# A two-block transformer kernel: two gate units move later in the mixture of experts, and the second attention mixer gets a written order with keys on partitions

## The chip, the core and the metric

The kernel runs on one core of one Trainium2 chip, in one launch. The metric is the device time of that launch in microseconds (us). A core has five engines that run side by side: TensorE (PE, matmuls and transposes; its weight loads are counted apart as PEld), VectorE (DVE), ScalarE (ACT), GpSimd (POOL) and SyncE (SP). SP issues nearly all the DMAs here, in the order of its own queue. Each engine takes its instructions in order; between engines they wait for semaphores.

## The reference, cut to what matters

The sequence has 512 tokens of 1024 features. Two blocks follow each other; the change is in the second, whose two layers are:

```python
for i in range(2):
    mix = even_mixer(x, ...) if i == 0 else odd_mixer(x, ...)
    x   = layer_norm(ALPHA * x + mix @ w_o[i], ln1_g[i], ln1_b[i])
    ffn = expert_choice_moe(x, router_w[i], w1[i], w3[i], w2[i])
    ple = sigmoid(x @ ple_gate_w[i] + ple_gate_b[i]) * (p[i] @ ple_w[i])
    x   = layer_norm(ALPHA * x + ffn + ple, ln2_g[i], ln2_b[i])

def odd_mixer(x):                     # 16 query heads, 4 key/value heads of 64
    q, k, v = split(x @ w_in)         # 1024, 256, 256 columns
    q, k = rope(rms_norm(q)), rope(rms_norm(k))       # per head
    return softmax(q @ k.T / 8) @ v                   # no mask, 512 x 512 scores per head

def expert_choice_moe(x):             # 16 experts, 64 tokens each
    gates, idx = top_k(softmax(x @ router_w).T, 64)
    y = (silu(x[idx] @ w1) * (x[idx] @ w3)) @ w2 * gates   # 1024 x 1024 weights
    return scatter_add(y, idx)
```

## The kernel before, in words

Precision: a float32 matrix is split into a high part (float32r, `whi`) and the rest (`wlo`); a product is then three fast matmuls (`mm3`, L227 to L229: high by high, low by high, high by low). `split` (L218, L221) casts on ACT and subtracts on DVE, or on POOL where `pool` is set or `self.every` divides the count. Matmuls on plain float32 operands (the `ss`, `rt`, `o` products, the expert products) are issued as two passes each, and a float32 operand that is only 64 columns wide lets two heads or two experts sit side by side in the array.

Nothing outside the experts has an order written out by hand. A scheduler with a timeline model orders each engine's instructions by their dependencies and their place in the code; only inside `experts` does `keep_order` chain the PE instructions in the order of the code.

**Experts (`experts`).** Per layer 8 pairs `pi` of experts run one after the other. Each pair is two halves of hidden columns (`half` 0 and 1), each with products `a1`, `a3` (L1647, tile `a`), then transposes `ht`, then two products `y`. The weights come in chunks of 1 MB (`chunk`, L1639), 24 per pair, into 8 rotating slots; a chunk's DMA can be issued when the slot's earlier chunk has been used. `gather` (L1664, tile `ga`) fetches the tokens of four experts, every second pair, by matmuls with one-hot matrices: 16 matmuls for two feature tiles `kk` that share one PSUM tile, with DVE (L1670) taking out `kk = 0` and ACT (L1668) `kk = 1`. `scatter` (L1685, L1686) adds the pair's output to the tokens. Six of the eight `ple` gate units (`unit`, 30 fast matmuls each, tiles `pg`, `pv`, with 0.5 MB of weights of their own) are set between the halves by two tables: `units_a` after half 0, `units_b` after half 1. `ef.close()` at the last pair gives back the memory of the units, and in layer 1 the last norm's gain and bias (`lng`, `lnb`) are then loaded there.

**Between the layers (`next_features`, L1394 to L1398).** 32 transposes bring the normed tokens to features on partitions; ACT applies gain and bias (`xf`), DVE casts to the high part (`h`) and subtracts (`l`), eight tiles. Each key or query projection (tile `qk`) needs all eight.

**Odd mixer (`odd_mixer`).** `normed_rope` projects 128 columns (two heads), squares (`sq`), sums by a matmul (`ss`, L1824), takes the root on ACT (`r`), scales (`z`), rotates by a matmul (`rt`, L1830), and adds the two rope terms on DVE and POOL (L1832 to L1834). There are two such for the keys and eight for the query pairs. `full_pair` is the attention of two heads with queries on partitions: scores `s` (two passes, L1002), their maximum on DVE (L1003), the exponential on ACT with the sum accumulated (L1004), the division on DVE (L281), 32 transposes `pt` (L1016), their copies out of PSUM, and the products `o` with the values (L1027). `xtok * G + Bb` (L1879, L1880) rebuilds the residual on POOL, one whole token tile per pair in the code for the first four pairs.

Of the kernel before, what the change touches and what calls it, by code (L numbers as in the profile page):

```python
# [11 lines left out]
F32 = mybir.dt.float32  # L12
# [20 lines left out]
def constants():  # L33
# [55 lines left out]
    c["before"] = before  # L89
    c["slot"] = np.tile(np.arange(64, dtype=f32)[None, :], (128, 1))  # L90
# [55 lines left out]
class K:  # L146
# [5 lines left out]
    def open(self, es):  # L152
# [12 lines left out]
        nc.sync.dma_start(self.norms, self.ins["norms"].rearrange("p (n k) -> p n k", n=5))  # L165
        eps = p.tile([128, 1], F32, name="eps")
# [142 lines left out]
    def program(self):  # L309
        with ExitStack() as es:  # L310
            self.open(es)
            self.wr = es.enter_context(self.pool("wr", 3))
            for l in range(2):
                with ExitStack() as eB, ExitStack() as eA:
# [11 lines left out]
                    else:  # L326
                        with self.pool("nfg", 1, side="right") as gp, self.pool("wh", 2) as self.wh:
                            w = self.ins["w_in_odd_2"][0]
                            self.every = 99
                            k0 = self.split(self.wcols(w, 1024, 128), True)  # L330
                            gain = self.next_features(gp, A)
                            self.odd_mixer(A, B, k0, *gain)
# [696 lines left out]

    def even_mixer(self, A, B):  # L1030
# [351 lines left out]
    def next_features(self, gp, A):  # L1382
# [3 lines left out]
        with self.pool("nf", 2) as p, self.pool("nfp", 3, PSUM) as pp:  # L1386
# [3 lines left out]
            G, Bb = self.ln_load(gp, 0, "ln2")  # L1390
            for k in range(8):
# [3 lines left out]
                f = p.tile([128, T], F32, name="xf")  # L1395
                nc.scalar.activation(f, ps, AF.Identity, scale=g[:, k:k + 1], bias=b[:, k:k + 1])
                nc.vector.tensor_copy(A[0][k], f)
                nc.vector.tensor_sub(A[1][k], f, A[0][k])  # L1398
        return G, Bb
# [175 lines left out]
    def keep_order(self, first):  # L1575

        nc, tc = self.nc, self.tc
        prev = None
        for i in nc.cur_bb.bb.instructions[first:]:
            if i.engine == nc.tensor.engine:  # L1580
                if prev is not None:
                    tc.add_manual_dep(i, prev.name, mybir.DependencyInfo(mybir.DependencyClass.NoSync, mybir.DependencyReason.DATA),
                                      reason="keep_order")
                prev = i

# [34 lines left out]
    def experts(self, l, xhl, aff, slT, slot, g, b, st, ef, r1, early):  # L1620
# [3 lines left out]
        with ExitStack() as es:  # L1624
# [31 lines left out]
            def gather(xg, OH, k2s):  # L1656

                for k2 in k2s:
                    ps = pp.tile([128, 2, 256], F32, name="ga", tag=("t", "y", "sc", "y")[k2])
                    for kk in range(2):  # L1660
# [6 lines left out]
                        if kk:  # L1667
                            nc.scalar.activation(xg[:, k], ps[:, kk], AF.Identity, scale=g[:, k:k + 1], bias=b[:, k:k + 1])  # L1668
                        else:
                            nc.vector.tensor_scalar(xg[:, k], ps[:, kk], g[:, k:k + 1], b[:, k:k + 1],  # L1670
                                                    op0=OP.mult, op1=OP.add)
# [121 lines left out]
    def odd_mixer(self, A, B, k0, G, Bb):  # L1793
# [3 lines left out]
        with ExitStack() as es:  # L1797
# [55 lines left out]
            for j in range(8):  # L1853
                if j == 2:
                    self.every = 1
# [46 lines left out]
```

## Time and profile before

| | us |
|---|---|
| median of 3 runs (lowest, highest) | 3506.03 (3505.88, 3511.51) |
| the profiled execution, its own time | 3509.84 |
| its span, first to last instruction | 3508.0 |
| experts of layer 0, from the first gather | 2128 to 2642 |
| between the layers and odd mixer | 2642 to 2885 |
| output product, norm, routing of layer 1 | 2885 to 2971 |
| experts of layer 1, from the first gather | 2971 to 3485 |

The page cuts the span into 40 slices of 88 us. A digit is the busy share in tenths. PE is near 9 almost everywhere, which by itself says little: matmuls overlap, and an engine that waits for data between them still looks busy. The DMA line tells the stages apart: low shares in the first two thirds, 9 in both stages of experts. PEclk is the granted clock of TensorE in tenths of full speed.

### The profile page before, as it was taken

Reading aid. Unit: us, or ns where it says so; the run is one execution under the profiler, and the core shown is the slowest. Engines: PE = TensorE matmul, PEld = TensorE weight load, DVE = VectorE, ACT = ScalarE, POOL = GpSimd, SP = SyncE. Lnnn points to the kernel's source line nnn. Section 1 sums busy time; section 2 is a strip of 40 time slices with the busy share of each in tenths; the row PEclk is TensorE's granted clock in tenths of the full one; section 3 lists DMA queues with packets and bytes.
Section 4 is the critical chain, followed back from the end, with each engine's and each line's share of the span. In section 5 each row is a group of like instructions: output and inputs, shape, how many; then the busy total and the mean of one; then the engine's idle time right before and its main releaser. Section 6 shows DMA issues by size and latency. Waiting matters only on the chain. (4 is left out here: it accounts for less than half of the span.)

```text
span 3508.0 us, 37612 instructions
## 1 busy us (share of the span) xinstructions
PE 3305.6 (94%) x15018; PEld 2155.8 (61%) x15018; DVE 1582.8 (45%) x2527; ACT 1070.3 (31%) x1933; POOL 510.7 (15%) x357
## 2 busy tenths in 40 slices
PE   8999999999999999999989889999997999999996
PEld 6666578888766657888866765344435657444342
DVE  6555463444555546344457753122216775211213
ACT  4333333223333333322355432011013553111011
POOL 2012121001101212100230423000003103100001
PEclk9999999999999999999999989999998998999998
DMA  5101132234210113233220225999992013899997
GB/s 183 48 25 61 37 110 81 96 96 137 75 60 13 61 36 106 77 96 96 90 86 3 72 102 227 407 412 386 417 421 85 28 43 113 366 408 378 421 407 301
DMA packets 223583, 584.85 MB, mean 167 GB/s; under 512 B 17584, under 2 KB 160304, under 8 KB 173232
## 3 DMA queue, kind: packets, MB, share of 16 engines
q1 hardware_dynamic: 222976, 581.66, 43.9%
q8 instruction: 118, 1.93, 0.2%
q10 hardware_dynamic: 432, 0.79, 0.1%
q14 instruction: 57, 0.47, 0.0%
HBM read 580.30 MB, written 2.10 MB: 166 GB/s over the span
## 5 line engine op out<-in xcount | busy, mean ns | idle before, releaser
L218 ACT CAST whi<-w 128x1024 fp32r<-128x1024 f32 (+1 forms) x312 | 311.2, 1003 | 731.7 <-PE mm L228 498.8
L1647 PE MATMUL a<-w,xg 128*64 128x512 f32 x2048 | 481.4, 600 | 42.2 <-DMA w<-in_w_dram 42.2
L227 PE MATMUL mm<-h,whi 128*128 128x512 f32 x1056 | 417.9, 396 | 4.8 <-ACT whi L218 4.1
L229 PE MATMUL mm<-h,wlo 128*128 128x512 f32 x1056 | 415.0, 394 | 0.4 <-POOL wlo L221 0.3
L228 PE MATMUL mm<-l,whi 128*128 128x512 f32 x1056 | 412.0, 390 | 0.0
L221 DVE TENSOR_TENSOR wlo<-w,whi 128x1024 fp32r<-128x1024 f32 (+1 forms) x237 | 306.4, 1297 | 233.8 <-ACT whi L218 232.5
L1647 PEld LDWEIGHTS a<-w,xg 128*64 128x64 f32 x2048 | 158.5, 138 | 348.6 <-issue 252.8
L221 POOL TENSOR_TENSOR wlo<-w,whi 128x1024 fp32r<-128x1024 f32 x75 | 166.2, 2218 | 642.4 <-ACT whi L218 445.0
L1647 PE MATMUL y<-w,hT 128*64 128x512 f32 x1024 | 226.3, 594 | 3.3 <-DMA w<-in_w_dram 3.3
L227 PEld LDWEIGHTS mm<-h,whi 128*128 128x128 f32 x1056 | 199.3, 189 | 48.1 <-ACT whi L218 5.3
L229 PEld LDWEIGHTS mm<-h,wlo 128*128 128x128 f32 x1056 | 199.0, 188 | 47.2 <-DVE wlo L221 1.0
L228 PEld LDWEIGHTS mm<-l,whi 128*128 128x128 f32 x1056 | 199.0, 188 | 44.7 <-issue 0.7
L602 DVE TENSOR_REDUCE mx<-s 128x1 f32<-128x128 f32 x192 | 93.3, 489 | 192.6 <-PE s L601 191.7
L1742 DVE SCALAR_TENSOR_TENSOR th<-th,a 128x512 f32<-128x512 f32 x32 | 22.0, 688 | 317.5 <-ACT th L1741 317.5
L1647 PEld LDWEIGHTS y<-w,hT 128*64 128x64 f32 x1024 | 72.4, 137 | 144.8 <-issue 136.3
L604 ACT ACTIVATE P<-s,mx 128x128 f32<-128x128 f32 x192 | 100.9, 527 | 174.5 <-DVE mx L602 162.3
L948 POOL TENSOR_TENSOR u<-u 128x512 f32<-128x512 f32 x64 | 66.6, 1040 | 521.4 <-ACT E L947 275.5
L1717 POOL TENSOR_TENSOR og<-OH,aff 128x512 f32<-128x512 f32 x16 | 16.8, 1047 | 764.2 <-DVE oT L1760 747.6
L1785 DVE SCALAR_TENSOR_TENSOR yl<-y,gate,yh 128x512 fp32r<-128x512 f32 x32 | 24.0, 751 | 223.3 <-ACT yh L1784 223.3
L959 DVE TENSOR_TENSOR y<-mm,r 128x512 f32<-128x512 f32 x64 | 44.2, 691 | 160.8 <-PE mm L229 160.8
L1741 ACT ACTIVATE th<-a 128x512 f32<-128x512 f32 x32 | 19.1, 597 | 319.8 <-PE a L1647 319.8
L621 PEld LDWEIGHTS pt<-c_ident,P 128*128 128x128 f32 x480 | 54.8, 145 | 73.1 <-issue 63.9
(584 smaller groups left out, 6414.2 us busy)
## 6 DMA issues: line engine op xcount, KB each, us to landing
w<-in_w_dram SPq DMA_DIRECT2D x384, 1024.0 KB, 12.6
w<-in_w_in_dram SPq DMA_DIRECT2D x32, 1024.0 KB, 5.3
w<-in_w_up_dram SPq DMA_DIRECT2D x32, 1024.0 KB, 5.5
w<-in_w_down_dram SPq DMA_DIRECT2D x32, 1024.0 KB, 5.1
w<-in_w_out_dram SPq DMA_DIRECT2D x8, 1024.0 KB, 5.2
w<-in_w_o_dram SPq DMA_DIRECT2D x8, 1024.0 KB, 4.7
w<-in_ple_gate_w_dram SPq DMA_DIRECT2D x16, 512.0 KB, 4.9
w<-in_w_in_even_dram SPq DMA_DIRECT2D x7, 1024.0 KB, 5.4
```

What stands on the lines that cost most here:

```text
L218: nc.scalar.copy(h, view)
L221: e.tensor_sub(l, view, h)
L227: mm(ps, wh, xh, start=first, stop=False)
L228: mm(ps, wh, xl, start=False, stop=False)
L229: mm(ps, wl, xh, start=False, stop=last)
L602: nc.vector.tensor_reduce(mx[:, i:i + 1], s[:, :n], axis=X, op=OP.max, negate=True)
L604: nc.scalar.activation(pv, s[:, :n], AF.Exp, bias=mx[:, i:i + 1], accum_out=sums[:, i:i + 1])
L621: nc.tensor.transpose(ps[:, (i - k) * 128:(i - k + 1) * 128], P[h][0][i][:, k * 128:(k + 1) * 128], C["ident"])
L948: nc.gpsimd.tensor_mul(u, u, u)
L959: nc.vector.tensor_mul(y, ps, r2)
L1647: nc.tensor.matmul(ps[64 * a:64 * a + 64], lhs(a, 4 * kc + k), cw[a][:, k], start=kc == 0 and k == 0, stop=kc == 1 and k == 3)
L1785: nc.vector.scalar_tensor_tensor(yl, y, gate, yh, op0=OP.mult, op1=OP.subtract)
```

## The change

1. **Gather.** DVE and ACT take out both halves of a gather tile after all 32 of its matmuls, not each after its own 16; the two engines change roles by name only.
2. **Gate units.** `units_a` goes from {0: 2, 3: 5} to {3: 4, 7: 7} and `units_b` from {0: 3, 2: 4, 4: 6, 6: 7} to {0: 2, 2: 3, 4: 5, 6: 6}: pair 0 has one unit instead of two, the last pair has one after its first half. The memory is given back after the last pair, and `lng`, `lnb` are loaded then.
3. **Between the layers.** Four PSUM tiles and four `xf` buffers; the casts `h` alternate between ACT and DVE; the residual scaling no longer stands here. The first key weights and the first query weights are both loaded and split ahead of it, on POOL. The two small norm gains are loaded at the program's start.
4. **Odd mixer.** Scores are computed twice: once with queries on partitions from the high parts only, for the maximum (`max_steps`), and once with keys on partitions (`attend_steps`), where the second pass carries the negative maximum in four spare rows. The exponential then gives the transposed weights directly; the sums come from adding the four key tiles (`acc`, two adds of three on POOL) and one matmul with ones; the division is done on the output, with a logarithm and an exponential on ACT. No transposes of the weights are left. `weave` sets the order of the steps from a string, and `keep_order` fixes it on PE.
5. **Residual.** Half a token tile per pair, all eight pairs, on POOL, each behind the output division of its pair.

```diff
@@ open
+        for g, n in zip(self.gqk, ("gqa_q_norm_2", "gqa_k_norm_2")):
+            for b in range(2):
+                nc.sync.dma_start(g[64 * b:64 * b + 64], self.ins[n][0].rearrange("(a b) -> a b", b=1))
@@ max_steps
+        def one(i):
+            s = pp.tile([128, T], F32, name="s", tag="s")
+            nc.tensor.matmul(s, q[:, 128 * i:128 * i + 128], k, start=True, stop=True)
+            nc.vector.tensor_reduce(mt[:, r0 + i:r0 + i + 1], s, axis=X, op=OP.max, negate=True)
+        def spread():
+            ps = pp.tile([128, 128], F32, name="mt", tag="mm")
+            nc.tensor.transpose(ps, mt, C["ident"])
+            rows = slice(r0, r0 + 4)
+            nc.vector.tensor_tensor(dst[rows]..., ps[rows, None, :]..., C["diag4"][rows]..., op=OP.mult)
@@ attend_steps
+        def score(h, k):
+            s = pp.tile([128, T], F32, name="st", tag="t")
+            for n, (kk, qq) in enumerate(passes[h]):
+                nc.tensor.matmul(s, kk[:, 128 * k:128 * k + 128], qq, start=n == 0, stop=n == len(passes[h]) - 1)
+            pt = PT[h, k] = at.tile([128, T], F32, name="PT", bufs=6)
+            nc.scalar.activation(pt, s, AF.Exp)
+            if k == 0:
+                acc[h] = at.tile([128, T], F32, name="acc")
+            else:
+                e = nc.vector if k == 3 else nc.gpsimd
+                e.tensor_add(acc[h], PT[h, 0] if k == 1 else acc[h], pt)
+        def norm():
+            nc.scalar.activation(r, sm, AF.Ln)
+            nc.scalar.activation(r, r, AF.Exp, scale=-1.0)
+            self.done = nc.vector.tensor_mul(r, r, o[0])
+            self.put_split(B, j, r)
@@ next_features
-            G, Bb = self.ln_load(gp, 0, "ln2")
-                nc.vector.tensor_copy(A[0][k], f)
+                (nc.vector.tensor_copy if k % 2 else nc.scalar.copy)(A[0][k], f)
@@ experts
-                        if kk:
-                            nc.scalar.activation(xg[:, k], ps[:, kk], AF.Identity, ...)
-                        else:
-                            nc.vector.tensor_scalar(xg[:, k], ps[:, kk], ...)
+                    k = 2 * k2
+                    nc.vector.tensor_scalar(xg[:, k], ps[:, 0], ...)
+                    nc.scalar.activation(xg[:, k + 1], ps[:, 1], AF.Identity, ...)
-            units_a, units_b = {0: 2, 3: 5}, {0: 3, 2: 4, 4: 6, 6: 7}
+            units_a, units_b = {3: 4, 7: 7}, {0: 2, 2: 3, 4: 5, 6: 6}
@@ odd_mixer
-                o = pp.tile([128, T], F32, name="o", tag="o", bufs=1)
-                self.full_pair(at, pp, o, passes, V)
-                self.put_split(B, j, o)
-                if j < 4:
-                    xt = self.xtok[:, j]
-                    nc.gpsimd.tensor_mul(xt, xt, G)
-                    nc.gpsimd.tensor_add(xt, xt, Bb)
+            self.weave("kkkkkkkk pp k pppppp k vvv p v k v p k v v vv", k=ks, p=p0, v=late)
+            self.weave("pp mp mp m mp mp mpp m m m p m", m=tops, p=steps[:9])
+                self.weave("pp r aa p aa pp mm aa p mm vv m m p aa p m vv mm p s s m kkkkkkkk kkkk", **chains)
+                s = slice(512 * (j % 2), 512 * (j % 2) + 512)
+                xt = self.xtok[:, j // 2, s]
+                m = nc.gpsimd.tensor_mul(xt, xt, G[:, s])
+                self.tc.add_manual_dep(m.ins, self.done.ins.name, ..., reason="residual")
+                nc.gpsimd.tensor_add(xt, xt, Bb[:, s])
```

In the strings p is one step of a query projection (eight triples of matmuls, then `ss`), r the rotation `rt` with the split of the next queries, a a score step, m a maximum step, v the values' product, s the sums and the division, k a step of the keys.

How the program's order moves, at three places. First SP, which issues the DMAs, in the experts of layer 1, last four pairs before and after (w is an expert chunk of 1 MB, `in_ple_gate` a unit's weights). Before:

```order
L1697 DMA w<-in_ple_gate_w_dram 128x1024
L1639 DMA w<-in_w_2_dram 128x2048 x48
L1697 DMA w<-in_ple_gate_w_dram 128x1024
L1639 DMA w<-in_w_2_dram 128x2048 x8
L1378 DMA lng<-in_ln_g_dram 128x1024
L1378 DMA lnb<-in_ln_b_dram 128x1024
L1639 DMA w<-in_w_2_dram 128x2048 x24
```

and in the change:

```order
L1773 DMA w<-in_ple_gate_w_dram 128x1024
L1717 DMA w<-in_w_2_dram 128x2048 x16
L1773 DMA w<-in_ple_gate_w_dram 128x1024
L1717 DMA w<-in_w_2_dram 128x2048 x8
L1469 DMA lng<-in_ln_g_dram 128x1024
L1469 DMA lnb<-in_ln_b_dram 128x1024
L1717 DMA w<-in_w_2_dram 128x2048 x8
```

The last pair's 24 chunks stood behind `lng` and `lnb`; now only its last 8 do, and a unit's weights stand between its first and second half.

Second, POOL from the end of layer 0's experts into the odd mixer (wlo is a split, z the rope term, xtok the residual). Before:

```order
L1717 TENSOR_TENSOR og<-OH,aff 128x512 x6
L221 TENSOR_TENSOR wlo<-w,whi 128x1024 x2
L1879 TENSOR_TENSOR xtok<-xtok,lng 128x1024 x4
L1880 TENSOR_TENSOR xtok<-xtok,lnb 128x1024 x4
L1833 TENSOR_TENSOR z<-z,c_gc 128x512 x2
```

and in the change, one pair of the loop (the third) on POOL:

```order
L228 TENSOR_TENSOR wlo<-w,whi 128x1024
L2022 TENSOR_TENSOR xtok<-xtok,lng 128x512
L1916 TENSOR_TENSOR z<-z,c_gc 128x512
L2025 TENSOR_TENSOR xtok<-xtok,lnb 128x512
L1969 CAST Q_17611<-z 64x512
L1969 CAST Q_17612<-z 64x512
L1097 TENSOR_TENSOR acc<-PT 128x512 x2
L1097 TENSOR_TENSOR acc<-acc,PT 128x512 x2
```

All eight residual instructions stood in one block ahead of the first rope; now two of them, at half the size, stand around each pair's rope term, and the adds of the sums are new behind them.

Third, PE in a pair of the odd mixer. Before, the piece around the fourth pair's sum of squares:

```order
L1016 MATMUL pt<-c_ident,P 128x128 x8
L1002 MATMUL s<-kh_17640,Q_18004 128x512
L1002 MATMUL s<-kl_17641,Q_18004 128x512
L1824 MATMUL ss<-sq,c_ones_17587 128x512
L1002 MATMUL s<-kh_17640,Q_18004 128x512
L1002 MATMUL s<-kl_17641,Q_18004 128x512
L1016 MATMUL pt<-c_ident,P 128x128 x4
L1027 MATMUL o<-PT,vo 64x256 x5
```

and in the change, the end of the second pair:

```order
L1069 MATMUL s<-kh_17772,Q_18088 128x512
L1103 MATMUL o<-PT,vo 64x512 x4
L1069 MATMUL s<-kh_17772,Q_18088 128x512 x2
L1906 MATMUL ss<-sq,c_ones_17596 128x512
L1108 MATMUL sm<-acc,ones 64x512 x2
L1074 MATMUL mt<-c_ident,mt_17601 128x128
```

The sum of squares `ss` is the same in both. The transposes `pt` are gone; the maximum's scores `s`, the sums `sm` and the small transposes `mt` are new, and nothing may pass them.

## Rows read from the trace of the kernel before

**Rows 1.** The page's 40 slices: granted clock and DMA share, in tenths.
```profile
PEclk9999999999999999999999989999998998999998
DMA  5101132234210113233220225999992013899997
```
**Rows 2.** Windows of the stages: busy us of each engine, granted clock, DMA share, GB/s.
```profile
2170.00:2642.00 472.00, 438.83 (x2034) 195.03 (x2030) 95.86 (x151) 52.17 (x88) 11.02 (x8) 1.00 0.99 406
2642.00:2709.00 67.00, 48.93 (x212) 36.19 (x211) 43.02 (x49) 23.76 (x39) 28.29 (x12) 0.77 0.16 50
2709.00:2885.00 176.00, 168.91 (x842) 105.69 (x840) 130.32 (x244) 102.56 (x219) 27.92 (x16) 0.99 0.11 37
```
**Rows 3.** Windows of 10 us in the experts, columns as before.
```profile
2150.00:2160.00 10.00, 10.00 (x48) 4.64 (x47) 1.38 (x2) 1.16 (x2) 3.10 (x3) 1.00 0.57 215
2160.00:2170.00 10.00, 10.00 (x49) 5.73 (x49) 2.67 (x4) 1.78 (x4) 1.05 (x1) 1.00 0.65 263
2250.00:2260.00 10.00, 10.00 (x49) 3.42 (x50) 0.75 (x1) 1.42 (x3) 0.00 (x0) 1.00 0.77 297
2380.00:2390.00 10.00, 9.68 (x50) 4.20 (x52) 0.42 (x2) 1.73 (x3) 0.00 (x0) 1.00 0.34 125
...
3220.00:3230.00 10.00, 8.72 (x55) 5.28 (x55) 1.09 (x2) 1.82 (x4) 0.00 (x0) 1.00 0.34 142
```
**Rows 4.** What PE waited for ahead of its gather matmuls (us, times).
```profile
  DVE xg L1670: 54.8, 64
```
**Rows 5.** PE in the experts of layer 0: start us, us, instruction, idle before.
```profile
2157.48 0.50 PE L227 MATMUL pg<-xfh,whi 128*128 128x512 f32 x1
...
2164.42 0.60 PE L1755 MATMUL ot<-c_ident,og 128*128 128x128 f32 x4
2164.95 13.95 PE L1647 MATMUL a<-w,xg 128*64 128x512 f32 x64
...
2602.51 15.01 PE L1647 MATMUL a<-w,xg 128*64 128x512 f32 x64
...
2623.81 3.65 PE L1647 MATMUL y<-w,hT 128*64 128x512 f32 x16 [0.35 <-DMA w<-in_w_dram]
2628.78 3.65 PE L1647 MATMUL y<-w,hT 128*64 128x512 f32 x14 [1.31 <-DMA w<-in_w_dram]
```
**Rows 6.** DVE between the layers: start us, us, instruction.
```profile
2657.53 0.42 DVE L1397 CAST h<-xf 128x512 fp32r<-128x512 f32 x1
2657.98 0.69 DVE L1398 TENSOR_TENSOR l<-xf,h 128x512 fp32r<-128x512 f32 x1
2658.59 2.58 DVE L1397 CAST h<-xf 128x512 fp32r<-128x512 f32 x1
2661.21 2.75 DVE L1398 TENSOR_TENSOR l<-xf,h 128x512 fp32r<-128x512 f32 x1
```
**Rows 7.** POOL between the layers and at one rope term.
```profile
2658.06 10.64 POOL L1879 TENSOR_TENSOR xtok<-xtok,lng 128x1024 f32<-128x1024 f32 x4 [5.94 <-PE xt L1394]
2668.66 10.35 POOL L1880 TENSOR_TENSOR xtok<-xtok,lnb 128x1024 f32<-128x1024 f32 x4
2685.82 1.29 POOL L1833 TENSOR_TENSOR z<-z,c_gc 128x512 f32<-128x512 f32 x1 [6.81 <-PE rt L1830]
```
**Rows 8.** PE at the first key projection's end, and single costs in the loop.
```profile
2675.13 0.63 PE L229 MATMUL qk<-h,wlo 128*128 128x512 f32 x1
...
2709.11 0.40 PE L1002 MATMUL s<-kl,Q 128*128 128x512 f32 x1
2709.35 0.40 PE L1002 MATMUL s<-kh,Q 128*128 128x512 f32 x1
...
2725.37 1.08 PE L1027 MATMUL o<-PT,vo 128*64 128x256 f32 x8
...
2745.02 1.02 PE L1824 MATMUL ss<-sq,c_ones 128*128 128x512 f32 x2
```
**Rows 9.** SP at the program's start.
```profile
1.66 0.43 SPq L291 DMA_DIRECT2D xT<-in_xT_dram  x1
```

More of the change, by code (lines that the diff above doesn't have):

```diff
@@ L1028, in full_pair, with weave @@
                                          start=k == 0, stop=k == 3)
+    def weave(self, plan, **chains):
+        at = dict.fromkeys(chains, 0)
+        first = len(self.nc.cur_bb.bb.instructions)
+        for c in plan:
+            steps = chains.get(c, [])
+            if c == " " or at.get(c, 0) >= len(steps):
+                continue
+            at[c] += 1
+            steps[at[c] - 1]()
+        assert all(at[c] == len(x) for c, x in chains.items()), (at, {c: len(x) for c, x in chains.items()})
+        self.keep_order(first)
@@ L1385, in next_features @@
         x = self.xtok
[L1386 removed]
+        with self.pool("nf", 2) as p, self.pool("nfp", 4, PSUM) as pp:
             cols = gp.tile([128, 16], F32, name="cols2")
@@ L1852, in odd_mixer @@
-            keys(0)
-            for j in range(8):
-                if j == 2:
-                    self.every = 1
-                if j == 3:
-                    keys(1)
-                if j % 2 == 0:
-                    raw = self.wcols(w, 128 * j)
-                z = normed_rope(raw[:, :, (j % 2) * 128:(j % 2) * 128 + 128], gq)
-                if j == 0:
-                    self.token_major(pp, w[:, 1280:1536], XH, XL, [v[:, t] for t in range(4)], one, "t")
+                z = []
+                steps = normed_rope((lambda: self.wcols(w, 1024 + 128 * j, 128)) if j else (lambda: first[0]), gk, z, "mm" if j else "s")
@@ L1863, in odd_mixer, with weights, project, queries @@
+            raws, zq, passes = {0: qw}, {}, {}
+            def weights(j):
+                if j % 2 == 0 and j:
+                    raws[0] = self.wcols(w, 128 * j)
+                return raws[0][:, :, (j % 2) * 128:(j % 2) * 128 + 128]
+            def project(j):
+                zq[j] = []
+                return normed_rope((lambda: weights(j)) if j else (lambda: first[1]), gq, zq[j], "mm" if j else "s")
+            def queries(j):
+                z = zq.pop(j)[0]
                 kh, kl = KS[j // 2]
-                passes = []
+                passes[j], steps = [], []
@@ L1872, in odd_mixer @@
+            tops = []
+            ks, p0, vs = keys(0), project(0), []
+            late = [lambda: vs.extend(values())] + [lambda t=t: vs[t]() for t in range(8)]
+            self.weave("kkkkkkkk pp k pppppp k vvv p v k v p k v v vv", k=ks, p=p0, v=late)
+            tops = queries(0)
+            steps = project(1)
+            self.weave("pp mp mp m mp mp mpp m m m p m", m=tops, p=steps[:9])
+            G, Bb = self.ln_load(gp, 0, "ln2")
+            for j in range(8):
                 g = j // 2
@@ new lines, in odd_mixer @@
+                if j < 7:
+                    turn, steps = steps[9], project(j + 2) if j < 6 else []
+                    tops = []
+                    chains["r"] = [lambda: (turn(), tops.extend(queries(j + 1)))]
+                    chains["m"] = [lambda i=i: tops[i]() for i in range(10)]
+                    chains["p"] = steps[:9]
+                if j == 1:
+                    chains["k"] = keys(1)
+                self.weave("pp r aa p aa pp mm aa p mm vv m m p aa p m vv mm p s s m kkkkkkkk kkkk", **chains)
```

169 lines of the change are left out of this document (114 added, 55 removed).

## The prediction

> **What bounds the kernel now.** I read the page's 40 slices first, because they tell the stages apart [rows 1]: the DMA share is 9 in two stretches, the experts of layer 0 and of layer 1, and low elsewhere. The windows by stage come next [rows 2]. In the experts the DMA engines are busy 0.99 of the time and move 406 GB/s; PE waits for weights there, and what counts is only when the DMA engines stand idle. In the odd mixer's pair loop (2709 to 2885) the DMA share is 0.11, the clock 0.99 and PE is busy 168.9 of 176.0 us: PE sets the time. Between the two (2642 to 2709) no engine is full, PE has 48.9 of 67.0 us and a granted clock of 0.77, so for nearly half of the stretch matmuls run at 1.2 GHz and not 2.4: a chain of waits sets it. So the change has three stages with three different limits, and I price each by its own.
>
> **Experts.** Windows of 10 us show where the DMA engines were idle in layer 0 [rows 3]: 4.3 and 3.5 us in the first pair (shares 0.57 and 0.65), 2.3 us at 2250, 6.6 us at 2380, together 16.7 us. Slots were full then and PE had not used them. Layer 1 shows the same dips, the deepest again 0.34.
>
> The gather waits are the first thing removed. PE waited 54.8 us for `xg` in 64 waits [rows 4]; a layer has 16 gather tiles, 32 in all, each seen once on PE and once on PEld, so a tile loses about 0.86 us and a gather of four tiles 3.4 us. Both halves now go out after both are filled, and the next tile is another one in PSUM, so this goes. It is worth something only where the DMA engines stood still: the 2.3 us at 2250 vanish, of the 6.6 us at 2380 about 3.2 remain (a unit at pair 2 and one at pair 3 still stand there).
>
> The unit after the first pair's first half is next. It ran from 2157.48 to 2164.42, 6.9 us [rows 5], exactly where the DMA engines had their first idle stretches. Without it and without the gather waits PE is some 11 us earlier there, and of 7.8 us idle I leave 1 us for the four chunks that the second gather delays. The first two gather tiles come before the DMA engines restart at all: 2 x 0.86 = 1.7 us more. Recovered per layer: 6.8 + 2.3 + 3.4 + 1.7 = 14.2 us.
>
> The same 6.9 us come back in the last pair. There the second half's products took 15.01 us against 13.95 us undisturbed, and PE waited 0.35 and 1.31 us in `y` [rows 5]: a slack of 2.7 us, so some 4.2 us of the unit show at the end of each layer. The unit's weights only change place in the DMA queue. In layer 1 `lng` and `lnb`, 1 MB together, no longer stand ahead of the last 24 chunks; two chunks, 2 MB, take 4.97 us there, so this is at most 2.5 us, and as PE sets the last pair then, I count 1 us. Sum for both layers: 2 x (14.2 - 4.2) + 1 = 21 us gained; bounds 6 (if only the first pair's idle time goes) and 30.
>
> **Between the layers.** DVE's cast took 0.42 us and its subtraction 0.69 us until POOL began the residual; from then on each took 2.58 and 2.75 us [rows 6], six of them in a row (three of each), while POOL did eight instructions in 10.64 + 10.35 us [rows 7]. The two engines took turns, one instruction each. The eight tiles cost DVE 5 x (0.42 + 0.69) + 3 x (2.58 + 2.75) = 21.5 us. The first key projection needs all eight tiles and ended at 2675.8 [rows 8]. In the change four casts are ACT's, the residual is gone from here, and DVE has 4 x 0.42 + 8 x 0.69 = 7.2 us in place of these 21.5. That would give 14 us. Two things take some back: POOL has both first splits and 24 memsets here, and ACT has twelve instructions in place of eight. I take 12 us; bounds 5 and 14. The rest up to the pair loop holds the same projections and the values' product, now in a written order; I count it as equal.
>
> The page SBUF — State Buffer of the Trainium skill, section Who interferes with whom, says that a DVE instruction with two SBUF inputs contends with a GpSimd instruction that reads SBUF, but not with one that only writes it. The turns of rows 6 and 7 agree with the first half; the second would let the memsets pass beside the subtractions, which speaks for the upper end, 14 us. The rule also speaks against this change, further on.
>
> **Pair loop.** First PE's own work, by single costs [rows 8]: a fast matmul of 512 columns starts 0.24 us after the one before, `ss` and `rt` take 1.02 us each, eight passes of `o` at 256 columns 1.08 us. A projection is 24 x 0.24 + 2 x 1.02 = 7.8 us. The loop of before held eight attentions, six query projections and one key projection: (176 - 7 x 7.8) / 8 = 15.2 us for an attention. In the change an attention has 16 fast score matmuls and 8 for the maximum (24 x 0.24 = 5.8 us), 16 passes of values at 512 columns (four times eight passes of half the width in pairs, 2 x 2 x 1.08 = 4.3 us), the sums 1.1 us, two small transposes about 0.4 us: 11.6 us. With its projection a pair is 19.4 us.
>
> Then what waits in the fixed order. The maximum's first scores stand about 6.9 us after the sums of the pair before. Ahead of them on POOL is now the residual's multiplication, which waits for the division of that pair (logarithm, exponential, product: about 2.2 us), then takes about 1.3 us, then the rope term 1.29 us [rows 7]; then DVE's add, ACT's cast and DVE's subtraction, some 0.65 us each, with POOL's second residual instruction of 1.3 us in front of DVE's add: 2.2 + 1.3 + 1.3 + 1.3 + 3 x 0.65 + 0.9 for the steps between = 9 us. So about 2 us of waiting per pair. Behind it PE can do nothing else, since its order is fixed. Six full pairs: 6 x (19.4 + 2) = 128.4; the second keys 7.8, and 4 for their `ss` and `rt`, which stand back to back with nothing between; the seventh pair without projection 11.6 + 2; the last 16 x 0.24 + 4.3 + 1.1 = 9.2, and 1.5 for the exponentials. Together 164.5 against 176, a gain of 11.5 us. Without any wait it would be 25.5, with 4 us per pair a loss of 2.5. The wait of 2 us is the nearest to the rows, as each of its links has one. The residual's eight blocks of two on POOL, 16 x 1.3 = 21 us in all, are otherwise hidden under PE.
>
> **Start.** Four small loads stand ahead of the first token tiles on SP, which takes about 0.45 us for each issue [rows 9]: 1.8 us lost, all of it on the path, since the first matmul waits for those tiles.
>
> **Sum.** 21 + 12 + 11.5 - 1.8 = 42.7 us. The profiled execution took 3509.84 us, 3.8 above the median 3506.03; taken from the median this gives 3463 us. The scheduler also moves instructions in the first block, which the change does not touch; I price that at nothing, with 5 us either way in the range.
>
> **Rivals.**
> 1. *The loop hangs on POOL.* POOL has about 13 us of work in a pair of 20, nearly all of it reading SBUF, and DVE's adds and subtractions on two SBUF operands then take turns with it, as in rows 6. If every one of six such DVE instructions waits 0.7 us more, the wait per pair is 6 us in place of 2, and the loop loses 7 x 4 = 28 us: 3491 us. For it: the turns are in the trace. Against it: DVE has 130 of 176 us now [rows 2] and loses the division and the copies. By the rule of the SBUF page named above this is what should come, for `acc` and the residual both read SBUF. Chance 0.2.
> 2. *The experts give back what they gain.* PE lags in the last pair by the whole unit and the first pair's idle time is set by its 8 slots, not by PE: the gain is 3 us per layer, 3478 us. For it: DMA share 0.99 in the stage. Against it: PE did wait for weights in that pair. Chance 0.15.
> 3. *The clock falls in the loop: slower.* Now PE runs at a granted clock of 0.99 there; in the stretch before, with its waits, it had 0.77 [rows 2]. A fixed order turns each late operand into a wait of all of PE. At half clock a pair's 19.4 us become nearly 39; more than two of the eight pairs at half clock eat the 42.7 us, and four give 3463 + 78 = 3541 us. Against it: waits of 1.31 us in `y` left the clock at full speed [rows 2]. Chance 0.07.
> 4. *No waits.* The written order hides the chain: 14 us more in the loop and 2 before it, 3447 us. Chance 0.2.
>
> The forecast itself has 0.38. About 0.2%, 7 us, is what can be told from no change here. Forecast and rivals 1, 2 and 4 are all faster by more than that, but their errors can reach it: faster 0.90, same 0.04, slower 0.06. The range from 3438 to 3494 holds the forecast's own errors (the bounds of each term) and rivals 1, 2 and 4.
>
> **What would show it.** In the experts: no wait for `xg` inside a gather, DMA shares near 1 from the first pair on, a dip left near the fourth pair, and the last pair's PE without waits for weights. Between the layers: casts at 0.4 and subtractions at 0.7 us, the first key projection ended some 12 us sooner after the last norm. In the loop: no `pt`, about 21 to 22 us from one `ss` to the next, one wait per pair, at the maximum's first `s`, put down to DVE's subtraction into `Q`. Wrong would be a loop of over 176 us, a clock under 0.95 in it, or idle DMA engines in the first pair.

## The result, and the profile after

The changed kernel takes 3450.65 us (median of 4 runs, 3446.95 to 3461.07), the kernel before 3505.95 us beside it; the ratio is 0.9845 with a 95% interval of 0.9818 to 0.9871, 55 us less. Measured once more with the last experiments it was 0.9838 (0.9820 to 0.9857). The forecast was 3463 us, so the sum came out 12 us short of the gain, and some of its terms were off by about as much or more, in both directions.

The profiled execution of after has a span of 3445.2 us, 62.8 below the 3508.0 of before. That is 7.5 more than the medians differ by: the one of before was 3.9 us above its median, the one of after 3.7 below. Cut at the same instructions of PE in both timelines (`affT` ends the routing ahead of a layer's experts, `a` is their first product with weights, `sc` the scatter of their output, `wo` the output product behind the mixer; all in us):

| stretch, by PE's instructions | before | after | gained | priced |
|---|---|---|---|---|
| to the first matmul | 9.1 | 12.1 | -3.0 | -1.8 |
| to the last `affT` of layer 0 (not touched by the change) | 2101.6 | 2089.9 | 11.7 | 0, 5 either way |
| to the first `a` of layer 0, and the same in layer 1 | 23.7 + 24.5 | 21.4 + 21.2 | 5.6 | in the next |
| experts to the last `sc`, layer 0 + layer 1 | 508.5 + 512.5 | 495.8 + 494.6 | 30.6 | 21 |
| last `sc` of layer 0 to the first key projection's end | 32.8 | 18.0 | 14.8 | 12 |
| from there to the first `wo` | 209.2 | 207.9 | 1.3 | 11.5 |
| output product and routing of layer 1, final norm | 86.1 | 84.3 | 1.8 | 0 |

First the page's two lines, which answer to [rows 1].

```profile
PEclk9999999999999999999999989999999999999998
DMA  5101132224310111233321115999994113999997
```

Of the clock's four 8s two are gone, those of slice 31 (between the layers) and of slice 34 (layer 1's routing). The DMA line has a 9 in the first slice of layer 1's experts, where it had an 8. Next the windows that answer to [rows 2] (busy us of PE, PEld, DVE, ACT, POOL; clock, DMA share, GB/s): the experts of layer 0, the stretch between, the pairs.

```profile
2149.00:2619.00 470.00, 440.00 (x2058) 197.74 (x2054) 99.09 (x156) 56.12 (x93) 13.30 (x9) 1.00 0.99 409
2619.00:2673.00 54.00, 43.99 (x221) 34.12 (x220) 32.94 (x52) 24.96 (x44) 22.54 (x31) 0.94 0.21 66
2673.00:2845.00 172.00, 150.87 (x563) 82.74 (x564) 109.53 (x146) 80.60 (x135) 99.58 (x75) 0.97 0.12 42
```

The experts move 409 GB/s in place of 406 at the same share of 0.99, since this window, like that of before, leaves the first pair's start out. The stretch between has a clock of 0.94 in place of 0.77. In the pairs PE's busy time fell from 168.9 of 176.0 to 150.9 of 172.0 us: the work fell by 18 us, the time by 4. POOL has 99.6 us there in place of 27.9.

Three windows of 10 us in layer 0's experts: the first pair, where [rows 3] had shares of 0.57 and 0.65, and two places in the fourth pair with a dip left (before, the deeper one was 0.34).

```profile
2143.00:2153.00 10.00, 10.00 (x50) 3.32 (x48) 1.54 (x2) 0.45 (x1) 1.07 (x2) 1.00 1.01 424
2330.00:2340.00 10.00, 10.00 (x49) 3.57 (x49) 1.45 (x3) 1.05 (x3) 1.05 (x1) 1.00 0.88 346
2350.00:2360.00 10.00, 10.00 (x64) 6.02 (x64) 1.63 (x3) 2.18 (x4) 0.00 (x0) 1.00 0.67 267
```

The first pair's share is full there. At the fourth pair's deeper dip 3.3 us are left idle, where 3.2 were foreseen; a dip of 1.2 us is new in the last pair (share 0.88 from 2580 to 2590), where a unit stands now. PE waits for no `xg` inside a gather any more. The last pair's products `y`:

```profile
2598.07 10.52 PE L1725 MATMUL y<-w,hT 128*64 128x512 f32 x48
```

48 products in one piece, without the waits of 0.35 and 1.31 us of [rows 5]: PE is later than the weights there, as foreseen. Between the layers, DVE (start us, us, instruction, idle before), which answers to [rows 6], and POOL beside it, to [rows 7]:

```profile
2627.98 0.43 DVE L1487 CAST h<-xf 128x512 fp32r<-128x512 f32 x1 [2.18 <-ACT xf L1486]
2628.44 0.69 DVE L1488 TENSOR_TENSOR l<-xf,h 128x512 fp32r<-128x512 f32 x1
...
2629.78 1.90 DVE L1488 TENSOR_TENSOR l<-xf,h 128x512 fp32r<-128x512 f32 x3
...
2633.55 0.78 DVE L1487 CAST h<-xf 128x512 fp32r<-128x512 f32 x1
2634.37 1.29 DVE L1488 TENSOR_TENSOR l<-xf,h 128x512 fp32r<-128x512 f32 x2
```

```profile
2633.56 0.92 POOL L1879 MEMSET mt<- 128x128 f32 x4 [12.16 <-issue]
2634.54 2.23 POOL L1925 MEMSET Q<- 64x512 f32 x4
```

Three of DVE's four casts take 0.43 us and the subtractions 0.63 to 0.69. Beside POOL's memsets (2633.56 to 2636.77) the fourth cast takes 0.78 us, and the last two subtractions take no longer than the others. Last, PE in an ordinary pair, and then in the seventh, the first that has no projection of a later pair between its steps:

```profile
2767.33 0.33 PE L1074 MATMUL mt<-c_ident,mt 128*128 128x128 f32 x1
...
2768.43 0.50 PE L234 MATMUL qk<-h,whi 128*128 128x512 f32 x1 [0.77 <-DVE Q L1076]
...
2775.94 0.73 PE L1069 MATMUL s<-kh,Q 128*128 128x512 f32 x2 [1.04 <-DVE Q L1968]
```

```profile
2809.28 0.33 PE L1074 MATMUL mt<-c_ident,mt 128*128 128x128 f32 x1 [0.55 <-ACT r L270]
...
2812.90 2.05 PE L1913 MATMUL rt<-z,c_rot 128*128 128x512 f32 x2 [3.28 <-DVE z L1910]
...
2813.96 1.42 PE L1090 MATMUL st<-Q,kh 128*128 128x512 f32 x1
...
2819.76 0.74 PE L1069 MATMUL s<-kh,Q 128*128 128x512 f32 x2 [1.25 <-DVE Q L1968]
```

An ordinary pair has the one foreseen wait at the maximum's first `s`, ended by DVE's subtraction into `Q`, and a smaller one at the first projection matmul, which wants the PSUM buffer that DVE's spreading of `mt` still reads. The pairs take 20.66, 20.67, 20.66 us from one `sm` to the next. The seventh takes 22.7 us although it has no projection's 24 matmuls and no `ss`, 6.8 us of PE work less. The record of granted clocks has 1.2 GHz from 2811.4 to 2818.3 there. It fell 1.8 us into the wait of 3.28 us: `rt` takes 2.05 in place of 1.02 us and the first `st` 1.42.

### The profile page after: what moved, and what is told of

Read it like the earlier page. It is cut to its first block, busy times and chain, and to the rows that moved or that the text cites. A ratio compares the mean times of both kernels' runs of the same rounds, so it can differ in the third digit from the quotient of the medians.

```text
span 3445.2 us, 37016 instructions
## 1 busy us (share of the span) xinstructions
PE 3255.6 (94%) x14746; PEld 2111.6 (61%) x14746; DVE 1553.8 (45%) x2435; ACT 1051.8 (31%) x1856; POOL 581.3 (17%) x437
## 5 line engine op out<-in xcount | busy, mean ns | idle before, releaser
L1817 ACT ACTIVATE th<-a 128x512 f32<-128x512 f32 x32 | 19.1, 597 | 341.6 <-PE a L1725 341.6
```

## The experiments

Each is read by its ratio to the kernel before, and by the same cuts as in the table above.

**1. The experts alone.** The kernel before, with these three edits.

```diff
-   if kk: nc.scalar.activation(xg[:, k], ps[:, kk], ...)                   # inside the loop over the halves
-   else:  nc.vector.tensor_scalar(xg[:, k], ps[:, kk], ...)
+   nc.vector.tensor_scalar(xg[:, k], ps[:, 0], ...)                        # behind the loop
+   nc.scalar.activation(xg[:, k + 1], ps[:, 1], ...)
-   units_a, units_b = {0: 2, 3: 5}, {0: 3, 2: 4, 4: 6, 6: 7}     # ef.close(), lng/lnb inside the last pair
+   units_a, units_b = {3: 4, 7: 7}, {0: 2, 2: 3, 4: 5, 6: 6}     # both behind the last pair
```

> The kernel before with the three edits in the experts alone (both halves of a gather tile go out after both are filled; the gate units' new pairs; the late closing of the pool with lng/lnb behind it). Theory from the two traces: the stage's gain is DMA idle time won back, nothing is lost in the last pair, and it needs nothing from the mixer: layer 0 from 508.5 to about 496 us, layer 1 from 531.3 to about 513 us, the first gather tiles some 2 us each; about 35 us in all, 3471 us, ratio 0.990. Rival, the sizes of the prediction: 21 us, 3485 us, ratio 0.994, with PE some 4 us late in each last pair. First two blocks: same order as before, so the times there differ from before only as two executions of one order differ.

Measured: 3467.92 us, ratio 0.9888 (0.9872 to 0.9905), 33 to 45 us. Layer 0 takes 495.95 us, layer 1 496.42. The theory's size holds; 21 us lies outside.

**2 and 3. Each half of it alone.** Gather only, then units with the late closing only.

> The kernel before with the gather edit alone (both halves of a tile filled, then both read). Both theories: no wait for xg inside a gather; the DMA dip of 2.3 us at the second gather goes, of the 6.6 us at the fourth pair about 3.2 stay, the first pair keeps most of its dip since its unit still stands there. About 9 us per layer, 18 us in all, 3488 us, ratio 0.995. If gather waits were covered by the weights' transfers: under 4 us in all, ratio above 0.999.

Measured: 3476.48 us, ratio 0.9911 (0.9896 to 0.9926), 26 to 36 us. The 18 us of both theories were too low.

> The kernel before with the new pairs of the gate units and the late closing alone; the gather as before. Theory from the traces: the first pair's unit of 6.9 us goes from a place where the DMA engines stood idle to a last pair where they set the time, so most of 5 us per layer is won and nothing given back: about 12 us, 3494 us, ratio 0.9966. Rival, the prediction's sizes: 5.1 us won and 4.2 us given back at the end of each layer, 1 us for lng/lnb: 3 us, ratio 0.999, with PE working on without a wait for weights in the last pair and the last products ending 4 us after the last chunk's usual time.

Measured: 3494.57 us, ratio 0.9966 (0.9953 to 0.9979), 7 to 16 us. The total is the theory's, but its places are not:

| kernel | layer 0 | its pairs 1 to 7 | its pair 8 | DMA idle before the last expert weight | from that weight to the end | layer 1 |
|---|---|---|---|---|---|---|
| before | 508.5 | 444.1 | 64.4 | 17.7 | 9.7 | 512.5 |
| gather only | 496.1 | 431.6 | 64.5 | 6.1 | 9.8 | 496.6 |
| units only | 508.0 | 440.0 | 68.0 | 14.8 | 10.5 | 505.1 |
| both, kernel before | 495.95 | 426.9 | 69.0 | 4.6 | 10.4 | 496.4 |
| the change | 495.75 | 426.8 | 69.0 | 4.4 | 10.3 | 494.6 |

(The pairs are cut at PE's first `a` of each. The idle time is the time from the first `a` of layer 0 to the last packet of an expert weight, less that of all DMA packets as a share of 16 engines.) The gather edit alone brings both layers to within 0.2 us of both edits together: on top of it the units' move is worth nothing in these cuts. PE reaches the last pair 4.7 us sooner and takes 4.5 us longer in it; of DMA time 1.5 us of idling are won and 1.3 given back, about half of it behind the last weight. The whole times do not show this nothing: experiment 1 is 8.6 us below experiment 2, with intervals that just overlap, and the ratios of 2 and 3 multiply to 0.9877, near the 0.9888 of 1. But the cuts repeat closely (layer 0 took 495.4 to 496.0 us in the nine profiles with both edits), and the scatter outside the experts, told under 9, is as large as those 8.6 us. Two windows of each, gather only and then units only, at the first pair and at the fourth:

```profile
2149.00:2159.00 10.00, 10.00 (x50) 6.04 (x50) 2.68 (x4) 1.78 (x4) 1.71 (x2) 1.00 0.69 286
2359.00:2369.00 10.00, 10.00 (x70) 7.13 (x70) 1.90 (x4) 2.75 (x5) 0.00 (x0) 1.00 0.74 305
```

```profile
2141.00:2151.00 10.00, 9.36 (x51) 4.22 (x50) 1.33 (x3) 1.73 (x3) 7.58 (x7) 1.00 0.76 302
2371.00:2381.00 10.00, 10.00 (x50) 3.35 (x48) 0.75 (x1) 1.01 (x2) 0.00 (x0) 1.00 0.59 222
```

With the gather edit and the unit left in the first pair, 3.1 us of that pair's dip remain, and 2.6 in the window at the fourth pair; with the units' move alone 2.4 us remain in the first pair, and 4.1 in one window of the fourth.

**4. The mixer alone.** The change with the three edits of 1 undone.

> The changed kernel with the three edits in the experts undone: the odd mixer, the residual and the four small loads at the start alone. From the last norm of layer 0 to the first output product of the next stage about 225 us against 242 before: 17 us. Theory A: the 8.7 us by which the changed kernel was ahead at the end of the first two blocks belong to its order there, which this kernel shares: 17 + 9 = 26 us, 3480 us, ratio 0.9926. Theory B: they were chance of one execution (fewer stretches at half clock), and only the 2 us of the start are left: 15 us, 3491 us, ratio 0.9957. The prediction's sizes were 12 + 11.5 - 1.8 = 21.7 us, ratio 0.994.

Measured: 3492.08 us, ratio 0.9962 (0.9948 to 0.9977), 8 to 18 us; 0.9888 x 0.9962 = 0.9850, so the two parts add up to the whole. From the last `sc` to the first `wo` it takes 228.5 us against 242.0. Nearer to B than to A.

**5. The seventh pair.** The next stage's first casts wait on ACT for the seventh pair's last exponential. They were suspected because of this in the change, on DVE:

```profile
2808.18 3.32 DVE L228 TENSOR_TENSOR wlo<-w,whi 128x1024 fp32r<-128x1024 f32 x2
2811.42 0.67 DVE L1076 TENSOR_TENSOR Q<-mt,c_diag 4x512 fp32r<-4x512 f32 x1
2812.02 0.73 DVE L1910 SCALAR_TENSOR_TENSOR z<-qk,gq,r 128x512 f32<-128x512 f32 x1
```

```diff
-   hl = [self.split(raws[...]) ...]
+   with self.tc.issue_after(self.gate6.ins): hl = [self.split(raws[...]) ...]      # l == 1, half == 0
```

> The changed kernel, with the first four casts of the next stage's output weights queued on ACT behind the last exponential of the seventh pair; nothing else. Theory S: the seventh pair lost its time to these four casts and to DVE's two subtractions beside POOL's third (3.32 us for two): they stand ahead of the maximum's spreading and of z, PE waits 3.28 us at rt, and then runs 7 us at half clock. Without them that pair takes about 16 us in place of 22.7, its half clock is gone, and from the first key projection's end to the first output product it is 202 us in place of 207.9; 6 us, 3445 us, ratio to before 0.983. Rival: with no projection left to fill PE's order the chain from the division to Q stands open anyway; the seventh pair stays above 20 us, or the casts delay the output products by as much, and the time stays at 3451 us.

Measured: 3459.95 us, ratio 0.9856 (0.9840 to 0.9872). Theory S fell: from key projection to `wo` it took 212.1 us, where it wanted 202. The seventh pair takes 22.97 us, the last 14.9 in place of 12.8. PE, then DVE:

```profile
2811.47 1.10 PE L1913 MATMUL rt<-z,c_rot 128*128 128x512 f32 x2 [1.52 <-DVE z L1910]
...
2818.54 0.74 PE L1069 MATMUL s<-kh,Q 128*128 128x512 f32 x2 [3.56 <-DVE Q L1968]
```

```profile
2815.08 1.74 DVE L1917 TENSOR_TENSOR z<-z,zs 128x512 f32<-128x512 f32 x1 [1.18 <-POOL z L1916]
2817.50 2.67 DVE L1968 TENSOR_TENSOR Q<-z,Q 64x512 fp32r<-64x512 f32 x2 [0.69 <-ACT Q L1967]
```

The wait at `rt` shrank from 3.28 to 1.52 us and the one at `s` grew from 1.25 to 3.56. With the 0.55 us ahead of `mt`, which is gone here, the waits add up to 5.08 us in both, since the chain from the sums to `Q` (8.8 us from 2809.7 to 2818.5) has only `rt` and eight `st` to cover it. DVE's rope sum takes 1.74 us beside POOL's residual and its subtractions 2.67 beside POOL's adds to `acc`, where in the change's seventh pair they take 0.69 and 1.70.

**6. The residual's dependency.** The change without it; the scheduler then puts the residual between the layers again.

```diff
-   self.tc.add_manual_dep(m.ins, self.done.ins.name, ..., reason="residual")
```

> The changed kernel without the residual's dependency on its pair; nothing else is edited. Its POOL work is then issued between the last norm and the first key projection again. Theory: DVE's subtractions there go back to some 2.7 us while POOL works, and the first key projection ends 8 to 12 us later after the last norm (26 to 30 us in place of 18.0), while the pair loop gets some 6 us shorter, since the residual's 2 x 1.3 us leave the chain from the division to Q (the wait of 1.04 us at the maximum's first s goes); net 2 to 6 us slower than the changed kernel, 3455 us, ratio to before 0.986. Rival: the stretch before the loop stays at 18 us because four casts are ACT's now, and the dependency was worth nothing; then the loop's gain is left and the kernel is 6 us faster, 3445 us, ratio 0.983.

Measured: 3467.73 us, ratio 0.9882 (0.9868 to 0.9895), which overlaps the change's first interval at the edge only and its second (0.9820 to 0.9857) not at all. The first key projection ends 28.9 us after the last `sc` in place of 18.0. DVE and POOL in that stretch:

```profile
2633.41 4.99 DVE L1488 TENSOR_TENSOR l<-xf,h 128x512 fp32r<-128x512 f32 x3
```

```profile
2634.46 6.50 POOL L2022 TENSOR_TENSOR xtok<-xtok,lng 128x512 f32<-128x512 f32 x4
```

Three subtractions of 1.66 us while POOL does four products of 1.63: the turns are back. So 10.9 of the 14.8 us are the dependency's. The other 4 are left for the four casts, the buffers and the earlier splits; no run takes these apart. The theory's other half failed: from key projection to `wo` it took 213.8 us in place of 207.9, and not 6 less. An ordinary pair takes 20.3 us in place of 20.67, and the seventh 26.8, with 26.8 us of half clock from the key projection to `wo` in place of 10.2.

**7 and 8. Taking the residual out of the chain, and a better order.** Both contain 5. In 7 a pair's residual is queued behind the next pair's `Q` copies on POOL. Its expectation's "pair after next" is the pair whose projections run beside it. In 8, besides: `mt` in the buffers of `s`, two more `a` ahead of the maximum, and the second keys' `ss` and `rt` inside the third pair.

```diff
-   "pp r aa p aa pp mm aa p mm vv m m p aa p m vv mm p s s m kkkkkkkk kkkk"
+   "pp r aa p aa pp aa mm p mm vv m m p aa p m vv mm p s s m kkkkkkkk"             # third pair:
+   "aa k aa r pp k aa kk p pp mm p mm vv m m p aa p m vv mm p s s m"
```

> The first of these with one more edit: each pair's residual is issued on POOL behind the Q copies of the pair after next in place of right behind its division. Theory: POOL's multiplication ahead of the rope term costs 1.3 us in the chain to Q, and DVE's rope sum takes 1.78 us in place of 0.69 beside POOL's add, both of which end in PE's wait of 1.04 us at the maximum's first s. With both gone the wait is gone and a pair takes 19.6 us in place of 20.67: 6 us below the first of these, 196 us from key projection to output product, 3439 us, ratio 0.981. Rival: the wait is then ended by ACT's cast or by POOL's rope term all the same, the period stays at 20.67 us, and the two kernels are equal.

> The one before with three edits of the written order: two more score tiles ahead of the maximum's first s, the transposed maximum in the buffers of s in place of those of the projection, and ss and rt of the second key projection inside the third pair in place of back to back behind the second. Theory: the wait of 0.77 us at each pair's first projection matmul goes, since it was ended by DVE's reading of mt in the same two buffers, and so do the 1.4 and 2.2 us at ss and rt: a period of 18.9 us, 5 + 4 = 9 us below the one before, 187 us from key projection to output product, 3430 us, ratio 0.978. Rival: the waits reappear at the next operand (the exponentials on ACT, the buffers of the scores), and the gain is under 3 us.

Measured: 3457.98 us, 0.9850 (0.9831 to 0.9868), and 3457.01 us, 0.9847 (0.9827 to 0.9866). Neither differs from the change. In 7 an ordinary pair of PE has no wait at `s`, but the sums come late:

```profile
2699.40 0.73 PE L1069 MATMUL s<-kh,Q 128*128 128x512 f32 x2
...
2711.03 2.02 PE L1108 MATMUL sm<-acc,ones 128*64 128x512 f32 x4
```

`sm` takes 2.02 us in place of 1.08, as its second half waits for DVE's last add, which waits for POOL's adds, which now stand behind the residual. The wait moved from `s` to `sm`, and from key projection to `wo` it took 210.8 us. In the time the rival holds, that the kernel equals that of 5. In 8 the waits of 0.77 us are gone, and pairs without a collision take 19.5 to 19.7 us; from key projection to `wo` it is 208.3 us all the same, since the last two pairs took 36.3 us in place of 35.5 and the second pair 21.9.

**9. The yardstick, and the first two blocks.** The change again, and the change with its four small loads back in the odd mixer (the first two blocks then have before's order on every engine).

> The changed kernel itself once more, as the yardstick for the two others of this call: 3451 us, ratio 0.9845; 2102 us to the last affT of layer 0, 18.0 us to the first key projection, 207.9 us from there to the first output product, the pairs at 20.67 us and the seventh at 22.7 us. If the seventh pair and the half clock there were chance, they differ here.

> The changed kernel with the four small loads of gq and gk, and the scaling of gq, back at the start of the odd mixer; the first two blocks then have the order of the kernel before, instruction by instruction. Theory: the change put another order there, and this is worth some 6 us net of the 2 to 3 us of a later first product: kernels with the order of before took 2107 to 2111 us to the last affT of layer 0, those with the new one 2102 to 2104; so 2108 us there, 3457 us in all. Rival, as predicted: the loads cost 1.8 us and the order is worth nothing; then 3449 us, and what the changed kernel won there was chance of the half-clock stretches.

Measured: 3454.34 us, 0.9838 (0.9820 to 0.9857), and 3455.56 us, 0.9849 (0.9835 to 0.9862). Not told apart. The seventh pair took 22.70 us again, so it is no chance. To the last `affT` of layer 0 the repeated change took 2108.7 us (2102.0 the first time), the other 2106.5. Over all profiles the new order took 2101.5 to 2110.0 us (eight), the old one 2106.5 to 2111.0 (five). The time goes with the half clock: 2101 to 2104 us where 95 to 96 us ran at 1.2 GHz, 2106 to 2110 at 105 to 109, 2111 at 116 to 122. So what the table shows there is for the larger part one execution's scatter; whether the new order is worth some 3 us on average stays open.

**10. A better place for the residual.** 8 with the residual behind POOL's last add of the next pair, where POOL stood idle, and DVE's first subtractions for the next stage behind the last spreading.

> The last of the four kernels before with two more edits: each pair's residual is issued on POOL behind the last of POOL's three-term sums of the pair after, where POOL stood idle, in place of behind the Q copies; and DVE's subtractions of the next stage's first weights are queued behind the last spreading of the maximum. Theory: the residual's 2.6 us then delay neither the chain to Q nor the sums, so neither s nor sm waits and a pair takes 18.8 to 19.6 us in place of 20.67; the seventh pair 17 to 20 us; 195 us from key projection to output product against 207.9; 3439 us, ratio 0.981. Rival: POOL and DVE are both nearly full along the pair's chain, a wait only moves on as it did from s to sm, and the stretch stays above 203 us.

Measured: 3450.20 us, ratio 0.9836 (0.9817 to 0.9856). PE in an ordinary pair:

```profile
2771.66 1.08 PE L1108 MATMUL sm<-acc,ones 128*64 128x512 f32 x4
...
2782.32 1.10 PE L1069 MATMUL s<-kh,Q 128*128 128x512 f32 x2 [0.26 <-DVE mt L1070]
```

`sm` no longer waits, and `s` waits only 0.26 us, for another operand; a pair takes 19.99 us, the seventh 19.1, and key projection to `wo` 202.0 us against 207.9 and 208.7. That is a shorter loop, half of what the theory wanted. In the whole time it does not show: 3450.2 against 3454.3 us of the change in the same measurement, with intervals that nearly coincide.

## Why the prediction was right, and which of its terms were not

**Experts, +21, got 36** (table) or 39, 33 to 45 (experiment 1): above the upper bound of 30. The step that failed most is "so some 4.2 us of the unit show at the end of each layer". PE's last pair did grow by as much (64.4 to 69.0 us in layer 0, 66.3 to 70.5 in layer 1). But the gain set against it was counted in idle time of the DMA engines, and in that account a layer loses only what is added behind its last weight: 0.6 and 0.4 us. PE had come to the last pair with a lead (the first seven pairs of layer 0 took 17.3 us less, for 13.3 us of idle time recovered). So 7.4 of the 8.4 us charged were not lost. The idle time itself was priced well in layer 0: 17.7 to 4.4 is 13.3 us, against 6.8 + 2.3 + 3.4 = 12.5. Layer 1, which was said to show the same dips, had more of it: 23.0 to 5.6, 4.9 us above that sum. The tiles ahead of the first `a` won 5.6 us in place of 3.4.

Inside the first pair the loss was divided wrongly. "A tile loses about 0.86 us" is the mean of 64 waits in [rows 4], and fits the later gathers, which take 11.5 us before and 7.8 to 7.9 in the change. (A gather tile has 16 matmuls, 8 for each half, and not 32 and 16 as said with the change.) But of PE's own 32 waits in before 28 are 0.64 us, two 0.71 and two 2.40. In the kernel before, the second half of layer 0's first gather took 9.06 us (2141.48 to 2150.54), where the change takes 4.0. Rows of before that the prediction did not look at, PE, then ACT and DVE:

```profile
2145.09 0.58 PE L1664 MATMUL ga<-OH,xkh 128*128 128x256 f32 x1 [2.40 <-DVE xg L1670]
...
2149.32 0.38 PE L1664 MATMUL ga<-OH,xkh 128*128 128x256 f32 x1 [0.64 <-DVE xg L1670]
```

```profile
2141.48 1.05 ACT L218 CAST whi<-w 128x1024 fp32r<-128x1024 f32 x1 [6.35 <-DMA w<-in_ple_gate_w_dram]
```

```profile
2142.56 2.02 DVE L221 TENSOR_TENSOR wlo<-w,whi 128x1024 fp32r<-128x1024 f32 x1 [9.31 <-ACT whi L218]
2144.50 0.53 DVE L1670 TENSOR_SCALAR xg<-ga,cols 128x256 f32<-128x256 f32 x1
```

The first wait is 2.40 us, because a weight split on DVE, 2.02 us beside POOL's work on the tokens, stood ahead of the evacuation. The granted clock was at 1.2 GHz from 2144.9 to 2148.3. The split is that of the unit's own weights, since the cast ahead of it waited for their DMA. With the unit moved and the gather left as it was (experiment 3) the same place reads:

```profile
2139.78 0.39 PE L1664 MATMUL ga<-OH,xkh 128*128 128x256 f32 x1 [0.64 <-DVE xg L1670]
```

The half gather takes 5.9 us there and 4.1 with the gather edit alone (experiment 2), both at full clock. So this loss goes with either edit, and what the two are worth can't be added. Alone, the gather edit was worth 26 to 36 us where its terms were 15, and the units' move 7 to 16; on top of the gather edit it brought nothing in the cuts, where its terms were 6. The other details held: the dip at the second gather gone, 3.3 us left at the fourth pair, PE later than the weights in the last.

**Between the layers, +12, got 14.8**, by the mechanism described; experiment 6 gives 10.9 of it to the residual's place. What was to take some back took little: POOL's splits were done by 2621.4, and the memsets came late, slowed one cast by 0.35 us and did not slow the subtractions. The page SBUF — State Buffer of the Trainium skill, section Who interferes with whom, says that a DVE instruction with two SBUF inputs does not contend with a GpSimd instruction that only writes SBUF. The rows of the two subtractions agree.

**Pair loop, +11.5, got 1 to 4.** The ordinary pairs were nearly right: 20.67 us with 1.8 us of waits against 19.4 + 2 = 21.4, PE's own work some 19.4 by experiment 10 (19.99 with 0.6 of waits). The failed step is "the seventh pair without projection 11.6 + 2". The 2 us are what is left of a 9 us chain (8.8 in experiment 5) when 6.9 us of PE work stand in front of it. In the seventh pair five projection steps of that work are gone, so the chain stands open: 5.1 us of waits, 6.8 us at half clock, and 22.7 us in place of 13.6. Of these 9.1 us the waits are 3.1 and the slower `rt` and `st` some 2.7 (5.6 us, estimated at 2.9 from the 1.02 and 0.23 us that they take in an ordinary pair); `rt` itself, 1.0 us, was left out of this pair's sum, and some 2 us are not accounted for. With the last pair (2.9 us over) and the second keys (1.2 over), less 5.7 under in the ordinary pairs, that is 172.0 in place of 164.5 us. The stretch ahead of it is 2.5 us longer than counted, as the first pair's maximum, eight matmuls, stands there and was in no sum.

**Start, -1.8, got -2.8** on average (11.9 us to the first matmul in eight profiles with the loads in front, 9.0 in five without).

**Rivals.** Rival 1 (the loop hangs on POOL) is true in kind and small in size: POOL and DVE take turns along the chain, 1 to 2 us per pair, and a wait taken away at one end comes up at the other (7). By the rule of that same page of the Trainium skill, that such a DVE instruction does contend with a GpSimd instruction that reads SBUF, this was to be expected, and the row of 1.74 us agrees. Rival 2 is refuted in the sum, but holds for the units' move on top of the gather edit. Rival 3 came true for 6.8 us in the seventh pair and 3.4 us at the second keys, but the loop as a whole stayed 4 us shorter than before. Rival 4 came nearest in time, 3447 us, for another reason: there were 26 us of waits.

So the number held because 10 us counted too much in the loop met 15 and 3 us counted too little in the experts and between the layers. That these nearly cancel is luck.

## What to carry to other kernels

A mean over waits hides the one that stands where it counts: list the waits inside the stretch that is priced, one by one, before multiplying. Where a stage is bound by transfers, count what a move gains and what it costs in the same account: here the idle time of the DMA engines and what is left behind the last transfer. In a fixed order a chain is hidden by the work in front of it, so price the iteration that lacks this work (the first, the last, the one before the last) by itself. Before moving work to an idle engine, find what queues behind it there, since in a full pair it only changes which wait is seen.

## What the runs showed that was not expected

- Four small loads at the start reorder the first two blocks on all engines, from PE's 38th instruction in the trace on, far from any other line that was edited.
- An untouched stretch of 2100 us varies by 8.5 us between executions of one order, with 95 to 109 us of it at 1.2 GHz. This is near the size of the terms of this change, so a stage is better compared by its own cuts than by the whole time.
- One DVE split of 2.02 us made PE wait 2.40 us, and the clock fell: half a gather took 9.1 us, without the split 5.9.
